# The seam of the second mixer and its FFN, and the first transfers, in another order: a two-layer encoder in fp32 on one core

## The chip, the cores and the metric

The kernel runs on one core of a Trainium2 chip, as one program. The metric is the device time of one execution in microseconds. The engines are PE (TensorE), DVE (VectorE), ACT (ScalarE), POOL (GpSimd) and SP (SyncE, which issues most of the DMAs).

## The reference

An encoder trunk of two layers on 1024 tokens of width 1024, in fp32. Layer 0 mixes with a windowed attention, layer 1 with a bidirectional gated linear recurrence (HGRN2, 8 heads of 128). Beside each mixer run 4 cross-attention heads into 256 memory tokens; both share one output projection. A gated FFN with a depthwise convolution follows. Norms stand before and behind each part.

```
mem_n = rmsnorm(mem, mem_norm_g)
for layer in range(2):
    u = rmsnorm(h, norm_g[layer, 0])
    mem_kv = mem_n @ w_mem_kv[layer]
    y = (mixer_window_attn, mixer_hgrn2)[layer](u, mem_kv, ...)   # concat([o, cross]) @ w_out
    h = h + rmsnorm(y, norm_g[layer, 1])
    gate, up = split(rmsnorm(h, norm_g[layer, 2]) @ w_in)          # 2 x 2816
    f = (gelu(dwconv3(gate) + b) * up) @ w_ffn_out
    h = h + rmsnorm(f, norm_g[layer, 3])
```

In `mixer_hgrn2` each head's output is normed with `norm_g`, multiplied by `silu(gate)` and then joined with the cross-attention heads ahead of `w_out`.

## The kernel before, in words

**Products.** Each fp32 product is three PE matmuls of fp32r halves: high by high, high by low, low by high (`mm3`, `mmk`; lines 81 to 83 and 557). A weight unit (`wunit`) is 128x1024: SP loads it into one of four stage buffers `st`, ACT casts the high half `wh` (line 86, 76 in the memory stage), DVE subtracts it to get the low half `wl` (line 87, 77). The ring holds four pairs of wh and wl. Activations lie as `uh`, `ul`, columns of the width on the partitions, tokens along the free dimension.

**Order.** The stages are written one after the other: memory keys and values (`start`), window attention (`window`), output projection of layer 0 (`wo0.finish`), FFN 0, HGRN (`hgrn`), output projection of layer 1 (`wo1.finish`), FFN 1. Which instruction stands where on an engine is not the order of the code: a scheduler with a simulated timeline interleaves all of it. `tc.high_priority` lifts instructions, and `tc.issue_after(x)` keeps the ones inside it behind x. Buffers come from pools, whose reuse makes waits per tile.

**The mixer's end.** `output(h, r, b, ...)` is called for both halves b of the tokens of each head. PE makes `po`; ACT, DVE and POOL norm it; DVE writes `on` (line 1255); PE turns it with four transposes into a PSUM bank `pt` (line 1259); for head 7 ACT and DVE write it into `uh` and `ul`.

**The output projection.** `Out.finish` goes over eight tiles of 128 tokens twice, in layer 1 in the order 4, 5, 6, 7, 0, 1, 2, 3. In the first pass (first 512 columns) a tile takes 12 `cross` matmuls (tiles `oh`, `ol`) and 6 `kept` ones (rows 6 and 7 of `uh`, `ul`). In the second pass it takes 36 into a bank `pb`; then ACT squares (line 100), DVE adds the residual into `x`, SP stores `x` to `h1d` (line 542), ACT squares again, DVE writes the normed rows `nu` (line 112), and PE turns them by eight transposes (line 116) into `uh` and `ul` for the FFN, through two banks `pt`.

**The FFN's start.** `plain(f)` computes the gate of the first weight block in bank X and the up part in Y, for tokens `ti` and then `tj`, 24 matmuls each. Beside it `operands` (a generator) builds on DVE and ACT sums of blocks of the activations, B[1] to B[7], which later products read; `u7h`, `u7l` are the seventh.

**The start.** `start` loads the memory columns `mT` (eight of 128x256) and the first weight unit in pieces, and scales and splits column by column (line 1351).

Of the kernel before, what the change touches and what calls it, by code (L numbers as in the profile page):

```python
# [47 lines left out]
def build(tc, A, out):  # L48
# [20 lines left out]
    def wunit(src, n=1024, pl=None, eng=None):  # L69

        tg = ("wh", "wl") if pl is None else ("xwh", "xwl")
# [8 lines left out]
    def mm3(o, ah, al, bh, bl, first, last):  # L80
        pe.matmul(o, ah, bh, start=first, stop=False)  # L81
        pe.matmul(o, ah, bl, start=False, stop=False)  # L82
        pe.matmul(o, al, bh, start=False, stop=last)  # L83
# [23 lines left out]
    def norm_T(pl, pst, src, g, dh, dl, t, tag="n"):  # L107
        ss = pl.tile([P, 1], F32, tag=tag + "ss", name=tag + "ss")
        u = pl.tile([P, D], F32, tag=tag + "u", name=tag + "u")
# [3 lines left out]
        for b in range(2):  # L113
            ps = pst.tile([P, 4, P], F32, tag="pt", name="pt")
            for k in range(4):
                pe.transpose(ps[:, k, :], u[:, (4 * b + k) * P:(4 * b + k + 1) * P], ident)  # L116
            split(dh[:, 4 * b:4 * b + 4, t * P:(t + 1) * P],
                  dl[:, 4 * b:4 * b + 4, t * P:(t + 1) * P], ps)
# [308 lines left out]
    class Out:  # L427

        def __init__(self, l, src, key, order):
            self.l, self.src, self.key, self.order = l, src, key, order  # L430
            self.us, self.wf, self.banks, self.used = {}, None, [], 0
            self.groups = (range(0, 6), range(8, 12), range(6, 8))
            self.units = (0, 1, 2, 4, 5, 3)
# [27 lines left out]
        def cross(self, ps, t, first, last):  # L461
# [5 lines left out]
            for i, k in enumerate(ks):  # L467
                wh, wl = self.us[self.b, k // 2]
                c = slice((k % 2) * 512, (k % 2 + 1) * 512)
                mm3(ps, oh[:, i, :], ol[:, i, :], wh[:, c], wl[:, c], first and i == 0, last and i == 3)  # L470
# [26 lines left out]
        def finish(self):  # L497
            l = self.l
            self.wf = tc.alloc_tile_pool(name=f"wf{l}", bufs=1, side="right", reuse_waits="tile") if l == 0 else None
# [7 lines left out]
            for i, t in enumerate(self.order):  # L507
# [4 lines left out]
                self.cross(ps, t, True, False)  # L512
# [12 lines left out]
            self.first = wunit(A["ffw1"][l, 0, :, :1024], pl=self.wf) if l == 0 else None  # L525
            for t in self.order:
                pool.tensor_tensor(y0[t], y0[t], g1[:, :512], op=ALU.mult)
            for t in self.order:
# [14 lines left out]
                norm_T(wp, psp, x, g2, uh, ul, t)  # L543
            psp.release()
# [16 lines left out]
    def ffn(l, wo, dst, gnext, halves_, out_halves):  # L561
# [35 lines left out]
        def plain(f):  # L597

            wg = wo.first if wo.first else wunit(A["ffw1"][l, f, :, :1024])
# [3 lines left out]
            def some(w, ps, ks, m, first):  # L603
                wh, wl = w
                mmk(ps, len(ks), lambda k: (wh[:, ks[k] * P:(ks[k] + 1) * P], wl[:, ks[k] * P:(ks[k] + 1) * P]),
                    lambda k: (uh[:, ks[k], m], ul[:, ks[k], m]), first)
            some(wg, gi, range(KT), ti, True)
# [13 lines left out]
        def operands():  # L621
# [263 lines left out]
        if wo.wf:  # L885
            wo.wf.release()
# [107 lines left out]
    def hgrn():  # L994
# [3 lines left out]
        early = tc.alloc_tile_pool(name="hg0", bufs=1, reuse_waits="tile")  # L998
        late = tc.alloc_tile_pool(name="hgv", bufs=1, side="right", reuse_waits="tile")
# [237 lines left out]
        def output(h, r, b, qin, S, As):  # L1237
# [15 lines left out]
            on = wp.tile([P, 4, P], F32, tag="on", bufs=1, name="on")  # L1253
# [3 lines left out]
            tp = bank("pt")  # L1257
            for c in range(4):
                pe.transpose(tp[:, c, :], on[:, c, :], ident)
# [264 lines left out]
```

## Time and profile before

| | |
|---|---|
| median of 3 runs | 2664.71 us (2661.21 to 2666.81) |
| profiled execution | 2661.84 us, of it 2659.7 in the span of the trace |
| busy PE, DVE, ACT, POOL | 2601.1, 1818.5, 1378.5, 469.6 us |
| mean granted clock of PE | 0.998 |
| moved by DMA | 425.93 MB, 160 GB/s on average |

How to read the rows that follow: a row of the timeline has the start in microseconds, the duration, the engine, the line of the kernel, the operation, out<-in with the shapes, the count, and in square brackets how long the engine had idled before and which instruction released it. A row of the windows has the stretch, its length, the busy time of PE, PE's weight loads, DVE, ACT and POOL (with the number of instructions), the granted clock of PE, the share of the DMA engines and GB/s.

### The profile page before, as it was taken

The numbers are of one execution on the slowest core, as the hardware profiler recorded it, in microseconds if no ns is written. First come the engines' busy times: TensorE is split into PE (matmuls) and PEld (weight loads), VectorE is DVE, ScalarE is ACT, GpSimd is POOL, SyncE is SP. The second block draws the span as 40 slices with busy tenths as digits, with TensorE's granted clock in tenths as the row PEclk, the third lists the DMA queues.
The fourth block names the chain that finished last, engine by engine and source line by source line (L and its number), as shares of the span: only waits on it lengthen the run. The fifth ranks groups of instructions, "written<-read, shape, count | busy, mean of one in ns | idle before, by whom it ended". The sixth has DMA issues, their size and how long they took to land.

```text
span 2659.7 us, 39101 instructions
## 1 busy us (share of the span) xinstructions
PE 2601.1 (98%) x14420; PEld 2184.7 (82%) x14420; DVE 1818.5 (68%) x3043; ACT 1378.5 (52%) x2503; POOL 469.6 (18%) x519
## 2 busy tenths in 40 slices
PE   8999999999999999999999999999999999999998
PEld 7888887788888888887888878888888788888887
DVE  6778886578655565478688686887757755656447
ACT  6467676545444445455464554555534444445443
POOL 0321010211111100031224131231211111110013
PEclk9999999999999999999999999999999999999999
DMA  9782232367777857674236351103436778775666
GB/s 354 247 172 57 74 90 82 103 190 193 199 202 193 210 153 257 191 249 150 84 112 153 82 124 52 52 25 103 134 124 178 193 193 209 198 203 166 225 191 237
DMA packets 195728, 425.93 MB, mean 160 GB/s; under 512 B 20048, under 2 KB 56272, under 8 KB 189904
## 3 DMA queue, kind: packets, MB, share of 16 engines
q1 hardware_dynamic: 161840, 325.11, 37.9%
q0 software_dynamic: 24544, 90.19, 16.4%
q10 hardware_dynamic: 9152, 8.14, 1.0%
q8 instruction: 113, 1.85, 0.3%
q14 instruction: 79, 0.65, 0.1%
HBM read 330.04 MB, written 116.39 MB: 168 GB/s over the span
## 4 chain that ended last, share of the span: by engine, by line
PE 82%; DVE 10%; ACT 3%; DMA 3%; issue 1%; POOL 1%; SPq 0%; ACTq 0%; DVEq 0%; POOLq 0%
PE X L557 29%; PE V L557 11%; PE pj L81 6%; PE pj L82 6%; PE pj L83 6%; PE Y L557 5%; PE pb L81 4%; PE pb L83 4%; PE pb L82 4%; DVE E L1146 1%; PE po L1249 1%; PE pt L383 1%; DVE ER L1181 1%; PE pt L116 1%; PE pu L1225 1%
## 5 line engine op out<-in xcount | busy, mean ns | idle before, releaser
L87 DVE TENSOR_TENSOR wl<-st,wh 128x1024 fp32r<-128x1024 f32 (+1 forms) x238 | 262.3, 1109 | 318.8 <-ACT wh L86 280.1
L86 ACT CAST wh<-st 128x1024 fp32r<-128x1024 f32 (+1 forms) x238 | 222.4, 937 | 287.6 <-PE X L557 190.3
L81 PE MATMUL pj<-uh,wh 128*128 128x512 f32 x512 | 202.9, 397 | 4.8 <-DVE q L1091 2.6
L557 PE MATMUL X<-wl,wh 128*128 128x512 f32 x528 | 204.7, 390 | 0.0
L557 PE MATMUL X<-wh,wl 128*128 128x512 f32 x528 | 204.6, 389 | 0.0
L82 PE MATMUL pj<-ul,wh 128*128 128x512 f32 x512 | 201.7, 394 | 0.1
L83 PE MATMUL pj<-uh,wl 128*128 128x512 f32 x512 | 201.7, 394 | 0.0
L557 PE MATMUL X<-wh 128*128 128x512 f32 x528 | 198.7, 390 | 0.9 <-ACT c L963 0.9
L81 PE MATMUL pj<-wh,uh 128*128 128x384 f32 (+1 forms) x512 | 189.7, 371 | 4.7 <-DVE gs L1077 2.5
L83 PE MATMUL pj<-wh,ul 128*128 128x384 f32 (+1 forms) x512 | 187.2, 366 | 0.0
L82 PE MATMUL pj<-wl,uh 128*128 128x384 f32 (+1 forms) x512 | 186.7, 365 | 0.0
L77 DVE TENSOR_TENSOR wl<-st,wh 128x1024 fp32r<-128x1024 f32 (+1 forms) x92 | 116.7, 1275 | 26.4 <-ACT wh L76 25.7
L557 PE MATMUL V<-uh,wh 128*128 128x512 f32 x344 | 133.8, 389 | 0.0
L557 PE MATMUL V<-ul,wh 128*128 128x512 f32 x344 | 133.8, 389 | 0.0
L557 PE MATMUL V<-uh,wl 128*128 128x512 f32 x344 | 133.8, 389 | 0.0
L76 ACT CAST wh<-st 128x1024 fp32r<-128x1024 f32 (+1 forms) x98 | 98.8, 1014 | 47.8 <-PE pj L82 25.4
L557 PEld LDWEIGHTS X<-wh 128*128 128x128 f32 x528 | 99.1, 188 | 21.9 <-ACT c L963 1.3
L81 PEld LDWEIGHTS pj<-uh,wh 128*128 128x128 f32 x512 | 96.3, 188 | 24.9 <-DVE q L1091 3.5
L557 PEld LDWEIGHTS X<-wl,wh 128*128 128x128 f32 x528 | 99.1, 188 | 20.7 <-DVE wl L87 0.3
L557 PEld LDWEIGHTS X<-wh,wl 128*128 128x128 f32 x528 | 99.1, 188 | 20.6
L932 POOL TENSOR_TENSOR c<-c,g 128x512 f32<-128x512 f32 x24 | 43.7, 1838 | 388.5 <-PE X L557 160.1
L83 PEld LDWEIGHTS pj<-uh,wl 128*128 128x128 f32 x512 | 96.2, 188 | 18.7
(399 smaller groups left out, 7212.6 us busy)
## 6 DMA issues: line engine op xcount, KB each, us to landing
st<-hid SPq DMA_DIRECT2D x154, 256.0 KB, 3.0
st<-in_ffw_dram SPq DMA_DIRECT2D x108, 256.0 KB, 3.1
w2s<-in_ffw_dram POOLq DMA_DIRECT2D x24, 1024.0 KB, 9.0
st<-in_ffw_dram SPq DMA_DIRECT2D x46, 512.0 KB, 4.4
hid<-tt SPq DMA_DIRECT2D x88, 256.0 KB, 4.8
st<-w2s SPq DMA_DIRECT2D x88, 256.0 KB, 3.4
sx<-in_ffw_dram SPq DMA_DIRECT2D x84, 256.0 KB, 3.9
sy<-in_ffw_dram SPq DMA_DIRECT2D x42, 512.0 KB, 6.9
```

The source lines that it names most:

```text
L76: act.copy(h[:, :n], raw)
L77: (eng or dve).tensor_tensor(l[:, :n], raw, h[:, :n].bitcast(F32), op=ALU.subtract)
L81: pe.matmul(o, ah, bh, start=first, stop=False)
L82: pe.matmul(o, ah, bl, start=False, stop=False)
L83: pe.matmul(o, al, bh, start=False, stop=last)
L86: act.copy(h, src)
L87: dve.tensor_tensor(l, src, h.bitcast(F32), op=ALU.subtract)
L116: pe.transpose(ps[:, k, :], u[:, (4 * b + k) * P:(4 * b + k + 1) * P], ident)
L383: pe.transpose(tp[:, j, :], sm[:, j, c * P:(c + 1) * P], ident)
L557: last = pe.matmul(o, x, y, start=new, stop=e, skip_group_check=not first)
L932: pool.tensor_tensor(y[q][:, t, :], y[q][:, t, :], g3[:, c], op=ALU.mult)
L1146: dve.tensor_tensor_scan(B[:, rev], smask, a_[:, rev], 0.0, op0=ALU.mult, op1=ALU.add)
```

## The change

It has four parts.

1. Mixer's end: for head 7 and the first half of the tokens, the last call of `output`, the four transposes of `on` and what follows them are kept as `wo1.last` and called in the first pass of `wo1.finish`, behind the third tile's cross products, with a bank of that stage. `on` and a copy of the gain (made on POOL) lie in a pool that lives on. The PSUM banks of the HGRN stage are laid out in another order.
2. Seam: in layer 1 the last two tiles (2 and 3) keep their `nu` in stage buffers; their transposes (`turn`) are issued behind the FFN's first gate product. The first gate unit of FFN 1 is loaded ahead into the space of `qin0` and `qin1` of the HGRN stage, which now come from a pool that is kept (`wo1.wf`).
3. `operands`, in both FFNs: the subtractions for the seventh operand also get the high priority.
4. Start: `mT` column 0 comes first on SP; columns 1 and 2 to 3 come on ACT's queue; the first weight unit comes in pieces of 256, 256 and 512 columns instead of 512 and 512, all on SP behind column 0.

```diff
-    def norm_T(pl, pst, src, g, dh, dl, t, tag="n"):
+    def norm_T(pl, pst, src, g, dh, dl, t, tag="n", kept=None):
         ss = pl.tile([P, 1], F32, tag=tag + "ss", name=tag + "ss")
-        u = pl.tile([P, D], F32, tag=tag + "u", name=tag + "u")
+        u = pl.tile([P, D], F32, tag=tag + "u", name=tag + "u") if kept is None else kept
         sumsq(pl, src, ss, u)
         rs = rstd_of(pl, ss, 1, D, tag)
         dve.scalar_tensor_tensor(u, src, rs[:, 0:1], g, op0=ALU.mult, op1=ALU.mult)
-        for b in range(2):
-            ps = pst.tile([P, 4, P], F32, tag="pt", name="pt")
-            for k in range(4):
-                pe.transpose(ps[:, k, :], u[:, (4 * b + k) * P:(4 * b + k + 1) * P], ident)
-            split(dh[:, 4 * b:4 * b + 4, t * P:(t + 1) * P],
-                  dl[:, 4 * b:4 * b + 4, t * P:(t + 1) * P], ps)
+
+        def turn():
+            for b in range(2):
+                ps = pst.tile([P, 4, P], F32, tag="pt", name="pt")
+                for k in range(4):
+                    pe.transpose(ps[:, k, :], u[:, (4 * b + k) * P:(4 * b + k + 1) * P], ident)
+                split(dh[:, 4 * b:4 * b + 4, t * P:(t + 1) * P],
+                      dl[:, 4 * b:4 * b + 4, t * P:(t + 1) * P], ps)
+
+        if kept is None:
+            turn()
+        return turn
...
+            if l == 0:
+                self.wf = tc.alloc_tile_pool(name=f"wf{l}", bufs=1, side="right", reuse_waits="tile")
...
+                crossed = self.cross(ps, t, True, False)
                 self.kept(ps, t, self.groups[2], False, True)
                 if t == self.order[5]:
                     after = self.last_read
+                if l == 1 and i == 2:
+                    with tc.issue_after(crossed.ins):
+                        self.last(psp.tile([P, 4, P], F32, tag="pt", name="pt"))
...
-            self.first = wunit(A["ffw1"][l, 0, :, :1024], pl=self.wf) if l == 0 else None
+            self.first = wunit(A["ffw1"][l, 0, :, :1024], pl=self.wf, tags=(None, ("qin0", "qin1"))[l])
...
-                norm_T(wp, psp, x, g2, uh, ul, t)
-            psp.release()
+                kept = stg.tile([P, D], F32, tag="st", name="nu") if l and t in self.order[6:] else None
+                turn = norm_T(wp, psp, x, g2, uh, ul, t, kept=kept)
+                if kept is not None:
+                    self.turns.append(turn)
+            if l:
+                self.pst = psp
+            else:
+                psp.release()
...
-            wg = wo.first if wo.first else wunit(A["ffw1"][l, f, :, :1024])
+            wg = wo.first
...
+            done = some(wg, gi, range(KT), ti, True)
+            for turn in wo.turns:
+                with tc.issue_after(done.ins):
+                    turn()
+            if wo.pst:
+                wo.pst.release()
...
-                more(q, x, B[1], kk, ALU.subtract)
                 with tc.high_priority(AHEAD):
+                    more(q, x, B[1], kk, ALU.subtract)
...
+        wo1.wf = tc.alloc_tile_pool(name="hgi", bufs=1, side="right", reuse_waits="tile")
...
-        for x in PB:
+        PA = [psp.tile([P, 4, P], F32, tag=f"pa{d}", bufs=1, name="pa") for d in range(2)]
+        for x in ("pu", "po", "pt"):
             bank(x)
-        PA = [psp.tile([P, 4, P], F32, tag=f"pa{d}", bufs=1, name="pa") for d in range(2)]
...
+            final = h == 7 and b == 0
+            on = (wo1.w1 if final else wp).tile([P, 4, P], F32, tag="on", bufs=1, name="on")
...
+            def turned(tp):
+                for c in range(4):
+                    pe.transpose(tp[:, c, :], on[:, c, :], ident)
+                return tp.rearrange("p c t -> p (c t)")
+
+            def last(tp):
+                tp = turned(tp)
+                oh, ol = (x[:, 7, b * 512:(b + 1) * 512] for x in (uh, ul))
+                act.activation(oh, tp, AF.Identity, scale=gain[:, 0:1])
+                dve.scalar_tensor_tensor(ol, tp, gain[:, 0:1], oh.bitcast(F32), op0=ALU.mult, op1=ALU.subtract)
+
             if h == 7:
-                tp = tp.rearrange("p c t -> p (c t)")
-                oh, ol = (x[:, 7, b * 512:(b + 1) * 512] for x in (uh, ul))
-                act.activation(oh, tp, AF.Identity, scale=bng[:, h:h + 1])
-                dve.scalar_tensor_tensor(ol, tp, bng[:, h:h + 1], oh.bitcast(F32), op0=ALU.mult, op1=ALU.subtract)
+                gain = wo1.w1.tile([P, 1], F32, tag="gain", bufs=1, name="gain") if final else bng[:, h:h + 1]
+                if final:
+                    pool.tensor_copy(gain, bng[:, h:h + 1])
+                    wo1.last = last
+                else:
+                    last(bank("pt"))
                 return
+            tp = turned(bank("pt")).rearrange("p (c t) -> p c t", t=P)
...
-            qin = [wp.tile([P, T], F32, tag=f"qin{d}", bufs=1, name="qin") for d in range(2)]
+            qin = [wo1.wf.tile([P, T], F32, tag=f"qin{d}", bufs=1, name="qin") for d in range(2)]
...
-        for k in (0, 2):
-            act.dma_start(mT[:, k:k + 2], A["memT"][:, k:k + 2])
+        nc.sync.dma_start(mT[:, 0:1], A["memT"][:, 0:1])
+        act.dma_start(mT[:, 1:2], A["memT"][:, 1:2])
+        act.dma_start(mT[:, 2:4], A["memT"][:, 2:4])
...
-        for p in range(2):
-            nc.sync.dma_start(raw0[:, p * 512:(p + 1) * 512], A["wmk"][0, 0, :, p * 512:(p + 1) * 512])
+        for c in (slice(0, 256), slice(256, 512), slice(512, 1024)):
+            nc.sync.dma_start(raw0[:, c], A["wmk"][0, 0, :, c])
```

On PE at the end of the mixer, before: the last four transposes of `on` stand ahead of the third tile's products.

```order
L83 MATMUL pb<-xwh,ul 128x512 x2
L1259 MATMUL pt<-ident,on 128x128 x4
L81 MATMUL pb<-wh,oh 128x512
L82 MATMUL pb<-wl,oh 128x512
L83 MATMUL pb<-wh,ol 128x512
```

The same place after the change, from the end of the third tile's products, of which 18 stand behind the row `L83 MATMUL pb<-xwh,ul 128x512 x2`:

```order
L82 MATMUL pb<-xwl,uh 128x512
L83 MATMUL pb<-xwh,ul 128x512
L81 MATMUL pb<-xwh,uh 128x512
L82 MATMUL pb<-xwl,uh 128x512
L83 MATMUL pb<-xwh,ul 128x512
L1283 MATMUL pt<-ident,on 128x128 x4
L81 MATMUL pb<-wh,oh 128x512
```

The four transposes have moved behind the third tile's 12 cross and 6 kept matmuls.

On PE at the seam, before: behind the last product of the output projection come the transposes of the tile before the last, and the first gate products of FFN 1.

```order
L83 MATMUL pb<-xwh,ol 128x512
L116 MATMUL pt<-ident,nu 128x128 x8
L557 MATMUL X<-uh,wh 128x512
L557 MATMUL X<-ul,wh 128x512
L557 MATMUL X<-uh,wl 128x512
```

The end of the gate product after the change (the qin tiles hold the weights, bank X the gate, bank Y the up part):

```order
L575 MATMUL X<-uh,qin_18727 128x512
L575 MATMUL X<-ul,qin_18727 128x512
L575 MATMUL X<-uh,qin_18728 128x512
L118 MATMUL pt<-ident,nu 128x128 x16
L575 MATMUL Y<-uh,wh 128x512
L575 MATMUL Y<-ul,wh 128x512
L575 MATMUL X<-uh,wh 128x512
```

The sixteen transposes of the last two tiles now stand in one row behind all 24 gate products; before, the last tile's eight stood behind the 24 up products and the first X of the next block. On SP the load of the up weights stood ahead of the last stores of `x` to `h1d`, and now stands behind the last of them.

On DVE in the second FFN, before, from the first of the two low halves of the seventh operand to the second:

```order
L87 TENSOR_TENSOR u7l<-tt,u7h 128x1024
L628 TENSOR_TENSOR c<-c,ul 128x1024
L87 TENSOR_TENSOR wl<-st,wh 128x512
L787 TENSOR_TENSOR u<-V,su 128x512
L628 TENSOR_TENSOR tt<-c,uh 128x1024
L87 TENSOR_TENSOR u4l<-c,u4h 128x1024
L628 TENSOR_TENSOR tt<-tt,ul 128x1024
L628 TENSOR_TENSOR c<-c,uh 128x1024
L87 TENSOR_TENSOR wl<-st,wh 128x512
L787 TENSOR_TENSOR u<-V,su 128x512
L87 TENSOR_TENSOR u7l<-tt,u7h 128x1024
```

The same after the change:

```order
L87 TENSOR_TENSOR u7l<-tt,u7h 128x1024
L651 TENSOR_TENSOR c<-c,ul 128x1024
L651 TENSOR_TENSOR tt<-c,uh 128x1024
L87 TENSOR_TENSOR u4l<-c,u4h 128x1024
L651 TENSOR_TENSOR tt<-tt,ul 128x1024
L651 TENSOR_TENSOR c<-c,uh 128x1024
L87 TENSOR_TENSOR wl<-st,wh 128x512
L810 TENSOR_TENSOR u<-V,su 128x512
L87 TENSOR_TENSOR u7l<-tt,u7h 128x1024
```

One pair of `wl` and `u` has moved from ahead of the second u7l to behind it.

More of the change, by code (lines that the diff above doesn't have):

```diff
@@ L67, in build, with wunit @@
     ul = up.tile([P, KT, T], F32R, name="ul")
[L69 to L71 removed]
+    def wunit(src, n=1024, pl=None, eng=None, tags=None):
+        tg = tags or (("wh", "wl") if pl is None else ("xwh", "xwl"))
         h = (pl or ring).tile([P, 1024], F32R, tag=tg[0], name=tg[0])
@@ L82, in mm3 @@
         pe.matmul(o, ah, bl, start=False, stop=False)
-        pe.matmul(o, al, bh, start=False, stop=last)
+        return pe.matmul(o, al, bh, start=False, stop=last)
     def split(h, l, src):
@@ L469, in cross @@
                 c = slice((k % 2) * 512, (k % 2 + 1) * 512)
-                mm3(ps, oh[:, i, :], ol[:, i, :], wh[:, c], wl[:, c], first and i == 0, last and i == 3)
+                done = mm3(ps, oh[:, i, :], ol[:, i, :], wh[:, c], wl[:, c], first and i == 0, last and i == 3)
+            return done
         def begin(self, psb, tags, y0, behind={}):
@@ L604, in some @@
                 wh, wl = w
-                mmk(ps, len(ks), lambda k: (wh[:, ks[k] * P:(ks[k] + 1) * P], wl[:, ks[k] * P:(ks[k] + 1) * P]),
-                    lambda k: (uh[:, ks[k], m], ul[:, ks[k], m]), first)
-            some(wg, gi, range(KT), ti, True)
+                return mmk(ps, len(ks), lambda k: (wh[:, ks[k] * P:(ks[k] + 1) * P], wl[:, ks[k] * P:(ks[k] + 1) * P]),
+                           lambda k: (uh[:, ks[k], m], ul[:, ks[k], m]), first)
+            done = some(wg, gi, range(KT), ti, True)
[4 more added lines that the diff above has]
+                wo.pst.release()
             some(wu, ui, range(KT), ti, True)
```

10 lines of the change are left out of this document (2 added, 8 removed).

## The prediction

> **What bounds the kernel now.** I read the page's busy shares and its chain first, then the waits of PE, then the stretches around each wait that the change touches.
>
> ```profile
> PE 2601.1 (98%) x14420; PEld 2184.7 (82%) x14420; DVE 1818.5 (68%) x3043; ACT 1378.5 (52%) x2503; POOL 469.6 (18%) x519
> PE 82%; DVE 10%; ACT 3%; DMA 3%; issue 1%; POOL 1%; SPq 0%; ACTq 0%; DVEq 0%; POOLq 0%
> ```
>
> PE is busy 98% of the span and carries 82% of the chain that ended last. The change adds or removes no matmul. So the whole question is what it does to PE's idle time, span 2659.7 less busy 2601.1 = 58.6 us at most, and to stretches in which PE's clock is cut. I take its places in order of size.
>
> **A. The last turn of the HGRN mixer.** What PE does there before the change, with the DVE step that it waits for:
>
> ```profile
> 1907.65 0.39 PE L81 MATMUL pb<-wh,oh 128*128 128x512 f32 x1
> 1909.46 0.39 PE L83 MATMUL pb<-xwh,ol 128*128 128x512 f32 x1
> 1910.38 0.60 PE L1259 MATMUL pt<-ident,on 128*128 128x128 f32 x4
> 1910.81 0.39 PE L1249 MATMUL po<-v,As 128*128 128x128 f32 x2
> 1916.58 1.12 DVE L1255 SCALAR_TENSOR_TENSOR on<-po,ors,gs 128x128 f32<-128x128 f32 x4 [0.60 <-POOL ors L93]
> 1917.08 1.16 PE L1259 MATMUL pt<-ident,on 128*128 128x128 f32 x4 [2.25 <-DVE on L1255]
> 1917.89 0.77 PE L81 MATMUL pb<-wh,oh 128*128 128x512 f32 x1
> 1920.59 0.42 PE L81 MATMUL pb<-xwh,oh 128*128 128x512 f32 x1
> 1916.00:1920.00 4.00, 2.92 (x9) 2.36 (x10) 1.87 (x5) 1.70 (x4) 0.90 (x2) 0.65 0.99 360
> ```
>
> PE stands 2.25 us before the four transposes, and the clock then granted is 0.65 (the last row, whose columns are the busy time of PE, PEld, DVE, ACT and POOL, the clock, the DMA share and GB/s). The price of that clock: the transposes take 0.81 us to the next start (1917.08 to 1917.89), where the same four took 0.43 a little earlier (1910.38 to 1910.81), so 0.4 more. The next six matmuls take 2.70 us (1917.89 to 1920.59). At full clock eight take 1.81 (1907.65 to 1909.46), 0.226 each, so six are 1.36: 1.3 more. Wait and slow clock together are 2.25 + 0.4 + 1.3 = 3.9 us.
>
> After the change 18 matmuls (the third tile's cross and kept products, 18 x 0.226 = 4.1 us) stand ahead of these transposes. They begin where the wait began, 1917.08 - 2.25 = 1914.8, and end at 1918.9. The normalized tile is complete at 1916.58 + 1.12 = 1917.7, so 1.2 us of cover is left and PE does not stop. The products that read the turned columns begin a further 18 matmuls on for the fourth tile and 12 cross products of the fifth, 6.8 us behind, which hides ACT's and DVE's split. The copy of the gain (one column, POOL) and the qin tiles that move to another pool cost nothing: POOL is busy 18%, and the first gate weights are not needed for another 100 us. **Term A: -3.9** (bounds -2.25, if only the wait goes, and -3.9).
>
> **B. The seam to the second FFN.** The second-half tiles end here; the last two tiles' steps before the change:
>
> ```profile
> 1996.58 0.60 ACT L100 ACTIVATE junk<-pb 128x512 bf16<-128x512 f32 x1 [2.71 <-PE pb L83]
> 2000.41 0.32 SPq L542 DMA_DIRECT2D h1d<-x  x1
> 2002.68 1.27 DVE L112 SCALAR_TENSOR_TENSOR nu<-x,nrs,g 128x1024 f32<-128x1024 f32 x1
> 2005.64 0.60 ACT L100 ACTIVATE junk<-pb 128x512 bf16<-128x512 f32 x1 [3.11 <-PE pb L83]
> 2010.61 0.33 SPq L662 DMA_DIRECT2D st<-in_ffw_dram  x1
> 2014.54 1.28 DVE L112 SCALAR_TENSOR_TENSOR nu<-x,nrs,g 128x1024 f32<-128x1024 f32 x1 [0.44 <-POOL nrs L93]
> 2015.02 1.04 ACT L86 CAST wh<-st 128x1024 fp32r<-128x1024 f32 x1 [2.71 <-DMA st<-in_ffw_dram]
> 2015.97 1.06 PE L116 MATMUL pt<-ident,nu 128*128 128x128 f32 x8 [1.37 <-DVE nu L112]
> 2028.03 1.04 PE L116 MATMUL pt<-ident,nu 128*128 128x128 f32 x8
> ```
>
> PE ends the last product at 2015.97 - 1.37 = 2014.6 and waits 1.37 us for the normalized rows of the tile before the last. The last tile's own transposes stand at 2028.03, well hidden. After the change the 24 gate products come first (24 x 0.226 = 5.4 us, to 2020.0), and then sixteen transposes in one row, of both last tiles. That is not free: the last tile's chain from its full bank to its rows took 2002.68 + 1.27 - 1996.58 = 7.4 us for a tile in calm and 2014.54 + 1.28 - 2005.64 = 10.2 for the crowded one. The last bank fills at 2014.6, so the rows are there at 2021.8 to 2022.0 by the calm price, while PE is through the first eight transposes (1.06 us) at 2021.1. DVE has further to empty the first tile's second bank, which is queued behind that step (half of a split, 0.7): about 1.9 us idle in all. Then the up products need their weights. Their load is now queued on SP behind the store of the last tile, which waits for x; the store came 2000.41 - 1996.58 = 3.8 us after the full bank, so the load goes at 2018.5. One such load took 2015.02 - 2010.61 = 4.4 us to its cast: 2022.9, and with the cast (1.04) and the next unit's behind it PE waits about 0.95 more. **B's wait: 2.85 - 1.37 = +1.5** (bounds -1.4, with no wait at all, and +4.3, with the crowded chain of 10.2).
>
> Does the clock fall too? The stretches in which PE idled tell what the next costs:
>
> ```profile
> 116.00:120.00 4.00, 2.30 (x10) 1.58 (x10) 3.91 (x10) 3.02 (x7) 2.22 (x4) 1.00 0.37 106
> 152.00:156.00 4.00, 1.87 (x12) 1.12 (x10) 3.94 (x11) 2.73 (x6) 2.07 (x3) 0.99 1.00 207
> 156.00:160.00 4.00, 3.94 (x13) 3.56 (x14) 3.73 (x12) 2.51 (x8) 0.00 (x0) 0.58 1.06 213
> 2068.00:2072.00 4.00, 2.34 (x11) 1.47 (x10) 4.00 (x6) 1.05 (x1) 0.22 (x1) 1.00 0.73 151
> ```
>
> With 1.70 us idle in 4 (116 to 120) and 1.66 (2068 to 2072) the clock stayed at 1.00. With 2.13 (152 to 156) it fell to 0.58 in the next 4 us, as after the 2.25 of A. B's 2.85 us, broken by a microsecond of transposes, lies above: I take the price of A's fall, 0.4 + 1.3 = **+1.7**, and B is +3.2 in all. The Trainium skill's page "TensorE: Matmul & The Clock Gate" (Part 1: The HAM clock gate) has the clock go cold only after at least one idle window of about 3.4 us. By that rule the fall after A's 2.25 us would not be there, and this case's trace has it; by the rule the 1.7 is not paid, which is a rival below.
>
> **C. The seventh operand of both FFNs.** Its two subtractions now go ahead of other DVE work.
>
> ```profile
> 2069.39 0.69 DVE L87 TENSOR_TENSOR wl<-st,wh 128x512 fp32r<-128x512 f32 x1
> 2070.59 1.22 DVE L87 TENSOR_TENSOR u7l<-tt,u7h 128x1024 fp32r<-128x1024 f32 x1
> 2071.86 0.50 PE L557 MATMUL X<-u7l,wh 128*128 128x512 f32 x1 [1.66 <-DVE u7l L87]
> 2075.47 0.50 PE L557 MATMUL Y<-uh,wl 128*128 128x512 f32 x1 [0.53 <-DVE wl L87]
> 630.13 1.05 ACT L86 CAST u4h<-c 128x1024 fp32r<-128x1024 f32 x1 [2.67 <-DVE c L628]
> 632.17 0.50 PE L557 MATMUL Y<-uh,wh 128*128 128x512 f32 x1 [0.60 <-ACT wh L86]
> ```
>
> PE idles 1.66 us for the second u7l and 0.53 for the weights behind it, 2.2 in the second FFN. One pair of other steps (2069.39 to 2070.59, 1.2 us) no longer stands ahead of u7l, and DVE begins its operand chain earlier against PE, since the last transposes move from 2028.03 to about 2022 while B puts PE 1.5 us later: 1.2 + 1.5 = 2.7 of cover for 1.66. **-2.2** (bounds -1.0 and -2.2). In the first FFN the cast that PE waits 0.60 for leaves its place behind the cast of u4h, which itself waits 2.67: **-0.3** (bounds -0.6 and +0.3).
>
> **D. The start.** First matmul, and the point at which the weights run short:
>
> ```profile
> 7.61 0.58 PE L81 MATMUL pb<-mh,wh 128*128 128x256 f32 x1 [7.61 <-ACT mh L1351]
> 16.51 1.05 ACT L76 CAST wh<-st 128x1024 fp32r<-128x1024 f32 x1 [1.07 <-DMA st<-in_wmk_dram]
> 21.18 1.21 DVE L77 TENSOR_TENSOR wl<-st,wh 128x1024 fp32r<-128x1024 f32 x1
> 22.47 0.48 PE L82 MATMUL pb<-wl,mh 128*128 128x512 f32 x1
> 8.00:13.00 5.00, 5.00 (x25) 4.87 (x25) 4.50 (x12) 4.90 (x11) 0.00 (x0) 1.00 1.04 411
> 17.00:22.00 5.00, 5.00 (x46) 5.00 (x45) 4.26 (x7) 4.25 (x6) 0.00 (x0) 1.00 1.03 410
> ```
>
> Smaller first pieces could bring the first matmul from 7.61 to about 4.6. But from 8 us on the transfers run at 411 and 410 GB/s with all engines taken (shares 1.04 and 1.03). The fourth weight unit's cast waits for its transfer at 16.51, and DVE ends a later weight unit at 21.18 + 1.21 = 22.39, 0.08 us before PE uses it at 22.47. Pieces that come earlier bring no bytes earlier: PE would start 3 us sooner and stand 3 us there. One more DMA and the two queues' new order are worth some tenths. **+0.2** (bounds -3.0, if it all comes through, and +0.7).
>
> **Attention.** In the first layer's window attention (163 to 230 us) the scheduler gives the same instructions another order, without any aim of the change.
>
> ```profile
> 64.00:163.00 99.00, 91.74 (x513) 83.53 (x513) 71.80 (x213) 54.38 (x136) 36.07 (x54) 0.98 0.82 233
> 163.00:232.00 69.00, 65.95 (x387) 59.30 (x386) 55.10 (x149) 45.74 (x119) 15.01 (x19) 1.00 0.55 122
> ```
>
> PE's idle time is the length less its busy time: 7.2 us in the 99 before, 3.0 in the 69 that are reordered. At the rate of the earlier stretch the 69 would have 5.0. I take 0, with bounds -2 and +2. One event like 152 to 160 costs more than that: 2.13 idle and 4 x (1 - 0.58) = 1.7 of clock, 3.8 us.
>
> **Sum.** -3.9 + 1.5 + 1.7 - 2.2 - 0.3 + 0.2 = -3.0 us. The profiled execution took 2661.84 (span 2659.7 and 2.1 around it), and would take 2658.8. The median of the runs shown is 2664.71, 2.9 above it and within their spread of 2661.21 to 2666.81. Against the median the sum gives 2661.7, 0.11% less. A measurement of this kernel can tell about 0.2% from no change, 5.3 us, so the forecast lies within that.
>
> **The rivals.**
> - *The seam stalls and the clock holds.* The 2.85 us come in pieces (1.9 and 0.95), each near the 1.70 and 1.66 that cost no clock. Against it stands 2.13 in 4 us, which did. Sum -4.7: 2660.0. This is also the result by the skill's rule named under B.
> - *No stall at the seam.* The last tile's rows come in time, if the scheduler's gap of 5.4 us of products and 1.06 of transposes covers a chain a little shorter than 7.4 us and the up weights land early. Then B is -1.4 instead of +3.2: sum -7.6, 2657.1. Against it: no such chain in the rows shown is under 7.4.
> - *The start comes through.* If the first pieces really fill idle transfer time (the first 8 us), D is -3.0 instead of +0.2: sum -6.2, 2658.5. Against it: 0.08 us of slack at 22.47.
> - *A crowded last tile.* The chain takes 10.2 us as in 2005.64 to 2015.82: 2.8 more, sum -0.2, 2664.5.
> - *Slower: attention stalls.* The reordered attention puts PE into waits as in 152 to 160, 3.8 us each. Two such events give +7.6, sum +4.6, 2669.3; it decides from a fraction of one event (3.0 us) on, and with three, 2673.1, it is out of the noise. For it: the attention before 163 us has such events; against it: in the 69 us reordered PE idles 3.0 in all, and the instructions are the same.
> - *The change does nothing of what it says*: excluded by the order of the instructions at A, B and C; at D it is the forecast itself.
>
> **How the numbers follow.** Chances: the forecast 0.30, no loss of clock 0.22, no stall 0.12, the start 0.10, the crowded tile 0.10, attention 0.16. Point: 2661.7. Faster by over 0.2% (below 2659.4) are no stall and the start (0.22), and, as terms of a microsecond or two are unsure, 0.40 of the no-loss case (0.09) and a sixth of the forecast (0.05): 0.36. Slower by over 0.2% (above 2670.0) is a good half of the attention case, which reaches it between two and three events: 0.10. Between them is 0.54. The range of 8 in 10 reaches from 2655.5, below no stall, to 2669.0, just under two attention events: outside are some 0.10 above and 0.07 below. The forecast's own range is 2659.2 to 2664.2.
>
> **What would show it.** Of the changed kernel: at the mixer's end, no wait at the transposes of on and no stretch with a clock under 0.9; at the seam, 24 products, then a wait of 1 to 3 us among sixteen transposes and another before the first up product, and the clock of the next 4 us; the wait of 1.66 at u7l gone; a first matmul near 4.6 us with waits of about 3 us before 25 us. Wrong it would be if a PE wait over 3 us stood at the seam or in 163 to 230 us, or if the first 30 us became shorter by 2 us or more.

## The result and the profile after

| | median | runs |
|---|---|---|
| before | 2663.80 us | 22 (2659.74 to 2667.73) |
| changed | 2667.51 us | 22 (2664.57 to 2670.98) |
| ratio | 1.0013 | 95% interval 1.0007 to 1.0018 |

The change costs 3.5 us (1.9 to 4.8 by the interval), where 3.0 less was forecast. The shares of the changed kernel's page:

```profile
PE 2608.7 (98%) x14420; PEld 2188.3 (82%) x14420; DVE 1818.4 (68%) x3043; ACT 1379.3 (52%) x2503; POOL 468.6 (18%) x520
PE 79%; DVE 12%; DMA 4%; ACT 3%; issue 1%; POOL 1%; SPq 0%; ACTq 0%; DVEq 0%; POOLq 0%
```

PE is busy 7.6 us longer with the same instructions, while its idle time, 2666.9 - 2608.7 = 58.2, is as before (58.6). So by these two sums most of this execution's loss is slow clock, which the rows below show behind waits. PE's timeline, its first matmul and then from the end of the mixer on:

```profile
5.74 0.58 PE L81 MATMUL pb<-mh,wh 128*128 128x256 f32 x1 [5.74 <-ACT mh L1387]
...
1924.04 0.70 PE L1283 MATMUL pt<-ident,on 128*128 128x128 f32 x4
2022.34 1.04 PE L118 MATMUL pt<-ident,nu 128*128 128x128 f32 x8
2024.83 1.26 PE L118 MATMUL pt<-ident,nu 128*128 128x128 f32 x8 [1.46 <-DVE ul L87]
2027.28 0.50 PE L575 MATMUL Y<-uh,wh 128*128 128x512 f32 x1 [1.20 <-ACT wh L76]
2029.86 0.79 PE L575 MATMUL X<-uh,wh 128*128 128x512 f32 x1 [1.84 <-ACT wh L86]
2035.57 0.41 PE L575 MATMUL Y<-ul,wh 128*128 128x512 f32 x1
2076.21 0.39 PE L575 MATMUL X<-u7l,wh 128*128 128x512 f32 x1
```

The wait of 2.25 us before the turned `on` is gone, and so is the one of 1.66 before `u7l`. In the waits of PE, grouped, 0.3 is left of all that it waited for u7l; it stands in the first FFN, at 630.78 us, where before had 0.25:

```profile
PE X L575 <- DVE u7l L87: 0.3, 1, 0.3
```

At the seam three waits, 4.50 us together, stand where one of 1.37 stood. Its windows (columns as in the prediction):

```profile
2024.00:2028.00 4.00, 1.97 (x10) 1.14 (x10) 1.37 (x3) 1.20 (x2) 0.00 (x0) 1.00 0.95 265
2028.00:2032.00 4.00, 2.16 (x6) 1.76 (x6) 3.02 (x5) 2.02 (x3) 0.97 (x1) 0.59 1.04 372
2032.00:2036.00 4.00, 4.00 (x11) 3.07 (x11) 4.00 (x6) 1.04 (x1) 0.14 (x2) 0.55 1.03 345
```

From 2029.86 to 2035.57 there are 13 starts in 5.71 us; at 0.226 each they would take 2.94: the clock costs 2.8 us there.

The attention, which the forecast left at nothing, has a new stall. ACT and PE of the changed kernel, and the window:

```profile
215.65 0.62 ACT L194 CAST kvh<-kvl 128x512 fp32r<-128x512 f32 x1 [5.76 <-DMA kvl<-kvd]
216.17 1.12 ACT L382 ACTIVATE sm<-sm,rd 128x384 f32<-128x384 f32 x2
216.84 2.05 PE L389 MATMUL pt<-ident,sm 128*128 128x128 f32 x8 [2.58 <-ACT sm L382]
216.00:220.00 4.00, 3.17 (x12) 2.61 (x12) 3.14 (x10) 3.11 (x10) 0.90 (x2) 0.57 0.18 68
```

PE's transposes wait for the scaled `sm`, which on ACT stands behind the cast of a cross head's memory keys, which waits 5.76 us for its load. The load and the transfer that was issued ahead of it, POOL and SP of the changed kernel:

```profile
206.81 0.87 POOL L142 DMA_DIRECT2D w2s<-w2s  x1
207.59 0.33 SPq L192 DMA_DIRECT2D kvl<-kvd  x1
```

and the same place before:

```profile
208.44 0.88 POOL L136 DMA_DIRECT2D w2s<-w2s  x1
208.96 0.33 SPq L186 DMA_DIRECT2D kvl<-kvd  x1
213.01 0.62 ACT L188 CAST kvh<-kvl 128x512 fp32r<-128x512 f32 x1 [1.83 <-DMA kvl<-kvd]
```

From its issue to the cast, the load of 256 KB takes 8.1 us (207.59 to 215.65) when POOL's transfer of 1 MB was issued 0.78 us ahead of it, and 4.1 when it was 0.52 ahead. The other traces repeat this: in all six executions with the stall the lead was 0.78 or 0.79 us and the load took 7.6 to 8.1; in the eight with this cast in its place and no stall the lead was 0.50 to 0.52 and the load took 3.1 to 4.1. The Trainium skill's page "DMA: Bandwidth & Descriptors" (Queues, rings and completion order) says that each DMA engine takes turns between its queues by whole packets; by that rule two such transfers share the engines. That fits a load that is slowed by the transfer beside it, but both kernels have that transfer; why the lead of 0.78 us costs twice the time of 0.52 is not shown.

To set the stretches side by side, each instruction of PE in a run was matched with the same one in before's execution. The table shows by how much the run fell behind (+) or gained (-) in each stretch (us of before):

| run | 0 to 28 | 160 to 232 | 232 to 500 | 1900 to 1930 | 1930 to 2012 | 2012 to 2136 |
|---|---|---|---|---|---|---|
| changed | +0.1 | +2.6 | +0.1 | -3.6 | +0.8 | +4.1 |
| changed, second execution | +0.1 | +2.6 | -0.1 | -3.6 | +0.8 | +2.8 |
| mixer's end alone | +0.4 | -0.5 | -0.1 | -3.7 | +0.8 | 0.0 |
| seam alone | -0.1 | -0.4 | 0.0 | +1.9 | 0.0 | +1.6 |
| start alone | -0.3 | +2.4 | +1.3 | +0.3 | 0.0 | 0.0 |
| without the seam | -0.1 | +2.9 | 0.0 | -3.3 | +0.8 | 0.0 |
| seam and mixer, early loads | 0.0 | +0.2 | -0.1 | -2.7 | +0.8 | +4.7 |
| whole change, early loads | +0.2 | +3.6 | +1.4 | -3.6 | +0.8 | +4.9 |

The changed kernel's two executions sum over these stretches to +4.1 and +2.6, about the measured 3.5. Their whole spans are 7.2 and 4.7 us longer than before's (2666.9 and 2664.4 against 2659.7); the rest lies in stretches that the table leaves out, 5.0 us of the first near 1866 us. Each row rests on one execution, so a difference of a microsecond in one cell can be chance.

### The profile page after: what moved, and what is told of

Same layout as the page of the kernel before. It is cut to its first block, busy times and chain, and to the rows that moved or that the text cites. A ratio compares the mean times of both kernels' runs of the same rounds, so it can differ in the third digit from the quotient of the medians.

```text
span 2666.9 us, 39120 instructions
## 1 busy us (share of the span) xinstructions
PE 2608.7 (98%) x14420; PEld 2188.3 (82%) x14420; DVE 1818.4 (68%) x3043; ACT 1379.3 (52%) x2503; POOL 468.6 (18%) x520
## 4 chain that ended last, share of the span: by engine, by line
PE 79%; DVE 12%; DMA 4%; ACT 3%; issue 1%; POOL 1%; SPq 0%; ACTq 0%; DVEq 0%; POOLq 0%
PE X L575 27%; PE V L575 11%; PE pj L81 6%; PE pj L82 6%; PE pj L83 5%; PE Y L575 5%; PE pb L83 4%; PE pb L82 4%; PE pb L81 4%; DVE E L1169 1%; PE pt L389 1%; DVE wl L77 1%; DVE ER L1204 1%; PE po L1272 1%; DVE wl L87 1%
## 5 line engine op out<-in xcount | busy, mean ns | idle before, releaser
L83 PE MATMUL pj<-uh,wl 128*128 128x512 f32 x512 | 201.7, 394 | 0.0
L83 PE MATMUL pj<-wh,ul 128*128 128x384 f32 (+1 forms) x512 | 186.8, 366 | 0.0
L83 PEld LDWEIGHTS pj<-uh,wl 128*128 128x128 f32 x512 | 96.2, 188 | 18.8
L82 PEld LDWEIGHTS pj<-ul,wh 128*128 128x128 f32 x512 | 96.3, 188 | 18.6 <-DVE ul L87 0.4
```

The lines of the kernel that those rows point to most:

```text
L83: return pe.matmul(o, al, bh, start=False, stop=last)
```

## The experiments

**One part at a time.** Each kernel has the parts of the diff that its name says, and the rest as before. Part 3 has no run of its own. The run without the seam has it, and there PE, DVE and ACT go through both FFNs in the order of the start alone, which lacks it.

Mixer's end alone.

> Only the mixer's end is changed (part 1). Theory S (the seam as built costs about 6 us, the late load of the up weights and of the next blocks behind the last store plus a clock fall; the mixer's end gains what it was to gain): time 3.5 to 4 us below before, no PE wait at the last transposes of on, clock 1.00 there, and the shift in the HGRN stage near 1866 us under 1 us. Rival H (the step of 5 us near 1866 us, PE waiting 3.1 us for ACT's ot, comes with the other bank layout or the kept pool of part 1): the step is there too, time +1 to +2 us.

Measured 2659.97 against 2663.95, ratio 0.9988 (0.9979 to 0.9997). No wait at `on`, no step near 1866 us. Theory S holds here.

Seam alone.

> Only the seam is changed (part 2). Theory S: +6 us, in PE waits of 1.2 to 2 us in sum 4 to 5 us around the sixteen transposes and the first up products, granted clock under 0.65 in the 4 to 8 us behind them; the wait of 1.66 us for u7l is gone although part 3 is not in. Rival H: the seam alone costs 1 us at most. Rival U (the u7l wait went because of part 3): that wait stays.

Measured 2667.49, ratio 1.0011 (1.0003 to 1.0020): half of the 6 us, and not all of it at the seam. From its timelines of DVE and PE:

```profile
1915.29 1.22 DVE L77 TENSOR_TENSOR qin<-st,qin 128x1024 fp32r<-128x1024 f32 x1 [0.36 <-ACT qin L76]
1919.47 0.75 PE L1278 MATMUL pt<-ident,on 128*128 128x128 f32 x3 [3.62 <-DVE on L1274]
2025.21 1.25 PE L118 MATMUL pt<-ident,nu 128*128 128x128 f32 x8 [1.46 <-DVE ul L87]
2027.48 0.50 PE L571 MATMUL Y<-uh,wh 128*128 128x512 f32 x1 [1.02 <-ACT wh L76]
2028.88 0.50 PE L571 MATMUL X<-uh,wh 128*128 128x512 f32 x1 [0.66 <-ACT wh L86]
```

The early split of the gate weights (`qin`) stands on ACT and DVE ahead of the last `on`, so that PE waits 3.62 us there instead of 2.25; with the mixer's end changed too, 18 matmuls stand between, and no wait at `on` is left. At the seam the waits sum to 3.1. The wait at u7l is gone without part 3, so rival U falls.

Start alone.

> Only the start is changed (part 4). Theory S: the first matmul comes 1.9 us earlier and all is given back by 28 us (+0.3), and the window attention is reordered with one stall of about 2.6 us and a clock fall near 215 us, +1.3; in all +1.6 us. Rival H says the same here. Rival N (the attention stall is noise of one execution): +0.3.

Measured 2666.95, ratio 1.0010 (1.0001 to 1.0019). The row of its PE timeline:

```profile
217.89 2.05 PE L383 MATMUL pt<-ident,sm 128*128 128x128 f32 x8 [2.35 <-ACT sm L376]
```

The stall is not noise: it was in all six executions that have the whole start and that cast in its place (2.11 to 2.58 us), and in none of the other twelve.

Without the seam.

> The change without the seam (parts 1, 3 and 4). Theory S: -3.5 for the mixer's end, +0.3 for the start, +1.3 for attention: about -2 us. Rival H: +2 to +3 us, since the step near 1866 us stays. Part 3 alone leaves every instruction where it was; if it does something here, the PE waits of 1.66 and 0.53 us at u7l are smaller.

Measured 2662.82 against 2663.95, ratio 0.9995 (0.9986 to 1.0004). The PE wait of 1.66 us at u7l stays, though part 3 is in:

```profile
2071.44 0.50 PE L561 MATMUL X<-u7l,wh 128*128 128x512 f32 x1 [1.66 <-DVE u7l L87]
```

**The step near 1866 us.** The first execution of the changed kernel lost 5 us more there: PE waited 3.10 us for ACT's `ot`, behind a late transfer. So the changed kernel was profiled once more:

> The changed kernel as it is, a second profiled execution. Theory S (its 5 us step near 1866 us, PE 3.1 us behind ACT's ot, is chance: a transfer of that execution landed late): the wait there is 0.5 to 1 us as in the four parts; the stall near 217 us and the three waits at the seam are there again. Theory H2 (the step comes only with all parts together): it is there again, about 5 us. Time +3 to +4 us by both.

Measured 2666.30, ratio 1.0010 (1.0001 to 1.0019). PE at that place, in the first and then in the second execution:

```profile
1869.21 1.11 PE L1243 MATMUL pt<-ident,ER 128*128 128x128 f32 x4 [3.10 <-ACT ot L1302]
```

```profile
1870.81 0.66 PE L1243 MATMUL pt<-ident,ER 128*128 128x128 f32 x4 [0.71 <-ACT ot L1302]
```

The step was chance: no later execution lost more than 1.0 us there. The stall at 217 us came again, and so did the seam's waits, as two (1.46 and 2.14 us) instead of three.

**Is the seam's cost the late load?** In the changed kernel the loads behind the seam are issued by SP only after the last store, which waits for `x` (its timelines of SP and ACT):

```profile
2011.67 9.47 SPq L554 DMA_DIRECT2D h1d<-x  x2
2021.19 1.30 SPq L75 DMA_DIRECT2D st<-in_ffw_dram  x1
2026.19 1.04 ACT L76 CAST wh<-st 128x1024 fp32r<-128x1024 f32 x1 [2.03 <-DMA st<-in_ffw_dram]
```

So both units were loaded where the gate weights are:

```diff
+ self.up = wunit(A["ffw1"][l, 0, :, 1024:])
+ self.a1 = stg.tile([P, 1024], F32, tag="st", name="st")
+ nc.sync.dma_start(self.a1, A["ffw1"][l, 1, :, 1024:])
...
```

With parts 1 and 2:

> Parts 1 and 2 without the start, and the second FFN's up weights and its next unit are loaded ahead of the stores of the last tiles, as the gate weights are. Theory S (the seam's cost is the late load, not the deferral itself): no PE wait over 0.5 us from 2000 to 2040 us and no clock under 0.9 there; -4.0 for the mixer's end as measured for it alone and -1.3 for the old seam wait, about -5 us in all. Rival T (sixteen transposes behind the gate product stall PE by themselves, through the last tile's chain): +1 to +3 us at the seam, 0 to -3 in all.

With the whole change:

> The whole change, with the second FFN's up weights and its next unit loaded ahead of the last stores. Theory S: against the changed kernel 5 to 6 us less (its three seam waits of 4.5 us go, and the fall of the clock with them), so -1 to -2 us against before. Rival T: +1 to +3 us at the seam stays, +1 to +3 against before.

Measured 2665.97, ratio 1.0003 (0.9993 to 1.0012), and 2668.38, ratio 1.0015 (1.0006 to 1.0023). The waits at the seam are gone in both; the scheduler then even spreads the sixteen transposes by itself. But the time is not. PE in the first of the two, and the window behind:

```profile
2070.59 0.50 PE L580 MATMUL X<-u7h,wh 128*128 128x512 f32 x1 [0.60 <-ACT su L816]
2074.19 0.73 PE L580 MATMUL X<-u7h,wh 128*128 128x512 f32 x2 [1.94 <-ACT u7h L86]
2076.58 0.80 PE L580 MATMUL X<-u7l,wh 128*128 128x512 f32 x1 [1.66 <-DVE u7l L87]
2076.00:2080.00 4.00, 3.42 (x8) 2.74 (x9) 1.89 (x3) 1.31 (x2) 0.00 (x0) 0.50 0.54 121
```

PE arrives earlier at the seventh operand and waits there, and the clock falls there. Both theories missed: the load did cause the seam's waits, but what the seam gives, the operand takes. The traces show why. POOL, ACT and DVE of the first of the two:

```profile
2029.85 0.97 POOL L697 DMA_DIRECT2D sx<-in_ffw_dram  x1 [7.61 <-PE pt L118]
2039.88 1.05 ACT L86 CAST wh<-sx 128x1024 fp32r<-128x1024 f32 x1 [7.40 <-DMA sx<-in_ffw_dram]
2040.97 1.23 DVE L87 TENSOR_TENSOR wl<-sx,wh 128x1024 fp32r<-128x1024 f32 x1 [5.34 <-ACT wh L86]
```

It is the pattern of the attention again: ACT's cast of the weights `sx` stands at the head of its queue and waits 7.40 us for a transfer that POOL issued (a load added into `sx`, 10 us from issue to cast), and DVE's next steps for the operands (`c<-c,tt` at 2042.11) stand behind it. Before, that step stood ahead of `wl<-sx` on DVE (2035.13 and 2042.09). In the second of the two ACT waits 7.23 us and DVE 4.92. So the second u7l begins no sooner on DVE: 59.2 us behind the first gate product (2016.12 to 2075.31), as in the changed kernel (59.3, 2016.73 to 2075.99). Before, it was 53.8 (2016.79 to 2070.59). No run brought `sx` in sooner or put that step ahead of it.

The last tile's transposes were then put behind half of the up product, which brings the operand chain forward:

```diff
- some(wu, ui, range(KT), ti, True)
+ some(wu, ui, range(KT // 2), ti, True)
+ with tc.issue_after(wo.turned.ins) if l else nullcontext():
+     some(wu, ui, range(KT // 2, KT), ti, False)
...
```

(and the first X product likewise). On the mixer's end alone:

> The mixer's end alone, and the transposes of the last tile put behind half of the FFN's up product instead of all of it and more; the loads stay as before. Theory O (the waits at u7l are set by the operand chain on DVE, which begins with those transposes): they come some 2.5 to 3 us earlier, the waits of 1.66 and 0.5 us at u7l and the weights behind are gone, 5.5 to 6 us under before (3.6 of it the mixer's end). Rival L (DVE and ACT are the limit there, whenever the chain begins): the waits stay near 2 us, time as with the mixer's end alone.

On parts 1 and 2 with early loads:

> Parts 1 and 2 with the early loads (as in the sixth run), and the last tile's transposes behind half of the up product. Theory O: no wait at the seam, and the waits of 0.6, 1.9 and 1.7 us at the seventh operand of the sixth run shrink to under 1 us with no clock fall: 6 to 7 us under before. Rival L: they stay at 3 us or more with the clock fall, time within 1 us of before.

Measured 2659.03, ratio 0.9986 (0.9977 to 0.9996), and 2662.86, ratio 0.9995 (0.9987 to 1.0004). At u7l the first still waits 1.14 of 1.66, and it gained 0.6 us from 2012 to 2136. PE in the second waits three times:

```profile
2068.02 0.50 PE L580 MATMUL X<-u7h,wh 128*128 128x512 f32 x1 [1.09 <-ACT su L819]
2070.49 0.50 PE L580 MATMUL X<-u7h,wh 128*128 128x512 f32 x1 [0.82 <-ACT u7h L86]
2072.42 0.50 PE L580 MATMUL X<-u7h,wh 128*128 128x512 f32 x1 [1.43 <-ACT su L819]
```

Theory O falls for the most part: the last tile's transposes came 2.9 us nearer to those of the tile before (9.1 us behind them instead of 12.1), and little of that reached u7l. Of L the waits came out in part (1.7 us in the first, 3.3 in the second), but not its reason. DVE was not busy throughout: in the second it stands 3.41 us behind the same late `sx`, for which ACT waits 10.13, and in the first 1.84 us behind ACT's `uh`, which waits 5.80 for PE's Y product. What limits the operands is a chain with a transfer in it, and which of its steps would have to go was not tried.

**The start.** Memory columns alone:

> Half of the start: the memory columns in their new order and queues, the first weight unit in two pieces as before. The window attention keeps its old order in this program. Theory S (the start's +3 us is the reordered attention, the start itself gives back its 1.9 us): time within 1 us of before, no stall near 217 us. Rival Q (the start itself costs, by queue order or one more transfer): +2 to +3 us.

Measured 2663.34 against 2663.66, ratio 0.9995 (0.9986 to 1.0004), with no stall at 217 us. Q falls. Then the whole start with the ACT casts moved; the last argument of `cross_head` is the instruction that a cast is queued after, `scaled_` holds the last scaling of sm on ACT:

```diff
- xhead[0] = cross_head(0, xh_, ea, None if xh_ else marks[0, 3])
+ xhead[0] = cross_head(0, xh_, ea, scaled_[0] if xh_ else marks[0, 3])
```

> The start alone (as in the third run), but ACT's cast of the cross heads' memory keys (kvh) is put behind the scaling of sm of the block before it, so that a late load of kvl no longer holds up sm on ACT. Theory K (the start's +3 us is this: PE waits 2.4 us for sm, which stands on ACT behind a cast whose load shares the DMA engines with a 1 MB transfer issued ahead of it, and the clock falls behind it): the wait near 217 us and the clock fall are gone, time within 1 us of before, about 3 us under the start alone. Rival Q (the start costs it elsewhere): still +2 to +3 us.

Measured 2668.45, ratio 1.0018 (1.0010 to 1.0027): the stall at 217 went (-1.5 from 160 to 232 us), but 7.9 us were lost from 232 to 500, so the time that theory K named was missed. Next, one head's cast only, by its number:

```diff
- xhead[0] = cross_head(0, xh_, ea, None if xh_ else marks[0, 3])
+ xhead[0] = cross_head(0, xh_, ea, {0: marks[0, 3], 2: scaled_[0]}.get(xh_))
```

> The start alone, with ACT's cast of the third cross head's memory keys behind the scaling of sm, the other heads' casts as in the start alone. Theory K: no PE wait of 2 us near 217 us, 3 us less than the start alone there (shift near 0 at 232 us); if the next head's cast makes no new wait, time within 1 us of before. Rival Q: 2 to 3 us above before with the stall gone.

This was the wrong head, the third. Measured 2669.89, ratio 1.0025 (1.0015 to 1.0034). PE in its timeline:

```profile
219.13 1.05 PE L383 MATMUL pt<-ident,sm 128*128 128x128 f32 x5 [2.23 <-ACT sm L376]
318.19 1.38 PE L383 MATMUL pt<-ident,sm 128*128 128x128 f32 x8 [1.17 <-ACT sm L376]
```

The stall at 217 stayed, and a new one stood at 318 us. The second head, whose cast stands at 217 us (1 for 2 in the edit):

> The start alone, with ACT's cast of the second cross head's memory keys, the one that stands near 217 us, behind the scaling of sm; the other heads' casts tied to nothing new. Theory K: no PE wait of 2 us near 217 us, the shift against before at 232 us within 1 us of that at 160 us; time within 1 us of before if the rest of the attention, which the scheduler lays out anew, makes no stall. Rival Q: the 2 to 3 us are there with the stall gone.

Measured 2660.47 against 2662.64, ratio 0.9992 (0.9983 to 1.0001): 0.0018 of the time, 4.8 us, under the start alone by the ratios, with no PE wait over 0.4 us from 160 to 228 us. ACT in its timeline scales sm at once:

```profile
212.47 1.12 ACT L376 ACTIVATE sm<-sm,rd 128x384 f32<-128x384 f32 x2
```

The cast itself now stands at 257.61 us, and the load behind POOL's transfer (issued 0.78 us ahead) is as late as ever. Theory K holds for the stall: it came from this one cast at the head of ACT's queue, and from 160 to 232 us this run gained 1.6 us where the start alone lost 2.4. Not all of the 4.8 us is that: the scheduler laid out the rest of the attention anew, and from 232 to 500 us the run gained 0.8 where the start alone lost 1.3.

**The slower matmuls of 1930 to 2012 us**, 0.8 us in every kernel with part 1. Part 1 with the banks of the HGRN stage laid out in the old order (`PA` behind the others):

> The mixer's end alone with the PSUM banks of the HGRN stage laid out as before; PE's order is the same as in the mixer's end alone. Theory M (the slower matmuls from 1922 to 2012 us come from which banks the products write): the shift stays flat there, 0.8 us less at 2012 us than with the new layout, unless the transposes then wait for a bank. Rival W (they come from something else, such as the pool that holds on): the shift grows by 0.8 us as before.

Measured 2659.66 against 2663.43, ratio 0.9988 (0.9979 to 0.9997), and again +0.8 to +0.9: M falls. The cause stays open.

**Together, without the seam.** Part 1, the earlier transposes and the one cast moved, with the start and without:

> The mixer's end, the last tile's transposes behind half of the up product, the start, and the cast near 217 us moved. If the parts add up: -3.6, -0.6 and -1 to -2, so 5 to 6 us under before. If the scheduler's new order of the attention makes other stalls, -3 to -4.

> The same without the start. If the start's own share is nothing (its 1.9 us given back by 28 us), the time is within 1 us of the run beside it; -4 to -6 us against before.

Measured 2659.91 against 2664.54, ratio 0.9981 (0.9972 to 0.9990), the lowest ratio of all, though its interval overlaps that of the mixer's end alone; and 2669.54, ratio 1.0016 (1.0007 to 1.0025). The first came out as the sum of its parts (5.1 us by the ratio), but not by its parts: the wait at u7l was back at 1.65 us in it and 1.66 in the second, so the 0.6 us of the earlier transposes did not repeat. The second was to be within 1 us of the first and came out 9.6 us above it by the medians. It lost 8.7 us from 232 to 500 us, in PE waits such as

```profile
316.95 0.50 PE L81 MATMUL pj<-uh,wh 128*128 128x512 f32 x1 [2.50 <-DVE xl L87]
```

Most of the difference lies there, in the attention order that the scheduler made with each, and not in the first 28 us, where the two differ by 0.3 us.

## Why the prediction was wrong

The forecast was 3.0 us less and the result is 3.5 more; the point of 2661.7 is 5.8 us off, though 2667.51 lies in the stated range.

- **Attention** was the step that failed: "I take 0". It is +2.6 us in both executions, one event of 2.58 us of wait and a clock of 0.57. The slower rival had named the place and the kind, with 3.8 us an event. It also said that a fraction of one event decides, and so it was: 2.6 us alone bring the sum to -0.4, and with the excess of B it is above 0. None of the signs named for being wrong came, since they asked for a wait over 3 us. What the argument lacked was a row of ACT: before the change it already idled 1.83 us for this load at the head of its queue. PE's waits alone showed nothing there.
- **B** was mis-sized in both terms. Waits: 4.50 - 1.37 = 3.1 instead of 1.5. The wait for the last tile came out as worked out (1.46 for the 1.9 named). The load did not: the working moved only the up weights behind the store, but the next units' loads moved with them, and the transfers run together (DMA share 0.95 to 1.04 from 2024 to 2036 us). The up weights took 5.0 us to their cast instead of 4.4 and PE waited 1.20 and 1.84 for two units instead of 0.95. Clock: 2.8 instead of 1.7, since the fall lasted 6.83 us and A's, from which it was priced, 3.41 (rows at the end). The rival by which the clock holds did not come about in either execution.
- **C** had the right size in the second FFN (2.2 idle, now none) and the wrong cause, so that the size is luck. Without the seam the wait stays though part 3 is in, and without part 3 it goes with the seam. It goes because PE comes later from the seam. DVE does not come earlier, as the working had it, but later: behind the first gate product its second u7l begins after 59.3 us instead of 53.8. So B's loss and C's gain are one account, and the rival "no stall at the seam" at -7.6 counted both: the two runs with early loads and no stall there lost 4.7 and 4.9 us in that stretch, and with the earlier transposes too it was still 0.8. Whether it would come about with `sx` in time is not shown. In the first FFN the 0.3 did not come: the wait of 0.60 for ACT's cast is gone, and one of 0.53 for DVE's `wl` stands in its place.
- **A** was right, in mechanism and size: 3.6 to 3.7 for 3.9, less 0.8 behind it that was not foreseen and is not explained.
- **D** was right at the start itself: 0.1 for 0.2, first matmul at 5.74 (4.6 named), all given back by 28 us, as the working said.

In sum, by the second execution: -3.6 + 0.8 + 2.8 + 2.6 + 0.1 = +2.7 us.

## What to carry to other kernels

Where a scheduler sets the order, a change at one place reorders others; look there for an engine whose queue is headed by an instruction that waits for a transfer, for it is one small shift away from stalling the next engine. Read the other engines' idle time for that, not only PE's: in these traces it is ACT's that shows the casts of `kvh` and of `sx`. A wait taken away pays only up to the next operand's readiness: price the chain of the other engines, transfers included, first. When one load is queued behind a store, look which others went with it.

## What was not expected of the hardware

The clock's fall is partly chance. The same waits of 0.48, 0.84 and 0.87 us stand from 153 to 156 us in before and in the changed kernel. Before, the clock fell to 0.58 in the next 4 us (row in the prediction); the changed kernel:

```profile
156.00:160.00 4.00, 3.49 (x18) 3.15 (x19) 3.94 (x12) 2.64 (x8) 0.00 (x0) 1.00 1.01 201
```

Windows that begin and end where the clock changed show what decides. Before, at this place and at the mixer's end:

```profile
152.54:155.95 3.41, 1.33 (x8) 0.72 (x6) 3.35 (x9) 2.17 (x5) 2.07 (x3) 1.00 1.04 216
1913.82:1917.23 3.41, 1.16 (x6) 0.61 (x4) 2.01 (x6) 1.18 (x7) 1.01 (x1) 1.00 0.80 201
1917.23:1920.64 3.41, 3.41 (x11) 2.67 (x11) 1.22 (x3) 2.02 (x5) 0.99 (x1) 0.50 0.95 386
```

The changed kernel, at this place and at the seam:

```profile
151.41:154.83 3.42, 2.32 (x15) 1.73 (x13) 3.42 (x8) 2.98 (x6) 1.84 (x3) 1.00 1.01 196
154.83:158.24 3.41, 2.23 (x10) 1.69 (x11) 3.34 (x11) 1.17 (x2) 0.23 (x1) 1.00 1.02 195
2025.33:2028.74 3.41, 1.49 (x8) 0.72 (x6) 0.04 (x1) 1.04 (x1) 0.00 (x0) 1.00 0.93 262
2028.74:2035.57 6.83, 5.71 (x13) 4.45 (x14) 6.59 (x8) 3.06 (x4) 0.97 (x1) 0.50 1.03 366
```

A fall is to half speed and lasts 3.41 us or, here, twice that. In each of the 18 executions all changes of the clock lie on one grid of 3.41 us, which lies elsewhere in the next execution. Before, the three waits fell into one window of that grid, with PE busy for 1.33 us of it, and the clock fell; in the changed kernel they fell into two, with 2.32 and 2.23 us, and it held. Counted over all 18 executions without their first and last microseconds, each of the 44 falls came behind a window with PE busy under 0.64 of it. Of the 28 windows with less than one half, 27 brought a fall; between one half and 0.64 both occur.

The Trainium skill's page "TensorE: Matmul & The Clock Gate" (Part 1: The HAM clock gate) says that the gate's window of about 3.4 us runs freely and does not start anew with the kernel; the grid agrees. That it takes a whole idle window to lose the clock does not agree: PE was busy for 1.16 us of the 3.41 ahead of the fall at 1917.23, and for 1.49 ahead of the one at 2028.74.
